# Eight half projections of the DeltaNet blocks moved into the filter stage, the second layer's modulations moved out of it

## The chip, the cores and the metric

The program runs on one core of a Trainium2 chip. Its engines are TensorE (PE in the profile; its weight loads are PEld), VectorE (DVE), ScalarE (ACT), GpSimd (POOL) and SyncE (SP), which here only issues DMAs. Each engine works through its own list of instructions in order, and semaphores tie the lists together. The metric is device time in microseconds (us) from start to end; lower is better.

## The reference, cut to what matters

Two layers over 1024 latent tokens of width 1024, with 256 context tokens in the first.

```python
def adaln_in(s, cvec, norm_g, mod_w, mod_b):
    m = jax.nn.silu(cvec) @ mod_w + mod_b
    shift, scale, gate = jnp.split(m, 3, axis=-1)
    return rmsnorm(s, norm_g) * (1.0 + scale) + shift, gate

def even_layer(x, ctx, ...):
    hx, gate_x = adaln_in(x, c_lat, norm_g, mod_w, mod_b)
    hc, gate_c = adaln_in(ctx, c_cx, norm_g, mod_w, mod_b)
    px = hx @ w_in
    pc = hc @ w_in
    ...
    dn_x, dn_c = bidir_gated_deltanet(px[..., OFF_DN:OFF_AB], ...)
    x_new = x + gate_x * ((jnp.concatenate([na_x, dn_x], axis=-1) * jax.nn.silu(px[..., OFF_Z:])) @ w_out)

def dn_prepare(qkv, ab, conv_w, a_log, dt_bias):
    t = jax.nn.silu(dwconv(qkv, conv_w)).astype(jnp.float32)
    ...

def hyena_layer(s, cvec, ...):
    h, gate = adaln_in(s, cvec, norm_g, mod_w, mod_b)
    ...
    filt = hyena_filters(s.shape[1], fw1, fb1, ff1, fw2, fb2, ff2, fw3)
```

The DeltaNet has four heads with a q, a k and a v block of 128 columns each: twelve column blocks of `w_in`, numbered 0 to 3 (q), 4 to 7 (k), 8 to 11 (v). k and v are also projected for the context tokens. The modulation `m` of a layer depends on `c` alone: a vector of 3072 numbers from a 1024 by 3072 matrix. The Hyena filters depend on weights alone.

## The kernel before

**Stages.** `start` (0 to about 378 us of the profile) computes the spectra of the Hyena filters, 16 of them, two for each column block `cb`: `filter_pair` multiplies (`fh`), scales and normalises; `filter_block` folds (`fp`, `ft`, `ff`) and transposes (`fx`); `filter_spectrum` makes the DFT on PE (`fb`) and stores the result (`G` to `g_d`). In the same stage the first layer's modulations (`em`), the normalised input h of tokens 0 to 511 and of the context, and at its end h of tokens 512 to 1023 are made. `project` (to about 740 us) makes the DeltaNet and attention projections: `gates` (`ab`), then for each head i `dn_front`, the gate block `zblock`, and for i = 1, 2 `dn_substitute` of the head before. Then come the DeltaNet scan (`dn_scan`, tiles `pa`, `pb`), attention, the output projection and the second layer.

**What sets the order.** Up to the end of the first part of `project` a scheduler orders the instructions of each engine by its own estimates; work in `high_priority(offset=-LOW)` is put where it leaves a hole. From the scan on, the matmuls are pinned in program order. All plain loads and stores stand on SP's one queue, and a DMA that waits holds up those behind it. POOL issues accumulating DMAs.

**Exact multiplication.** A weight block of 512 KB is loaded (`_raw`), split in `load_split` into a rounded part `hi` (a cast on ACT) and a remainder `lo`, and `gemm` takes three matmuls for each of eight slices of the contraction: 24 matmuls, of 512 columns for half of the latent tokens and of 256 for the context. With `add=True` the remainder is made by ACT (a negated copy) and an accumulating DMA from POOL (L154 to L156), otherwise by a subtraction on DVE. The buffers `wraw`, `whi` and `wlo` have two copies each.

**The modulation block.** `mod_block` (`em` and `om`, twelve blocks each) loads two halves of 512 KB, makes eight 32x256 matmuls into `_ps`, copies to `_p`, and for j below 8 transposes twice (`_t`) and reduces on DVE into `cols`; for j from 8 on one matmul (`_g`), an addition and a store to `gate_d`. Before, the twelve `om` blocks stand among the work of low priority in `start`, after eight `zblock`s; their loads use `wraw`, `whi` and `wlo`. `cols1` and `gate_d[1]` are first read after the scan.

**The DeltaNet block.** `dn_block` splits its weights, multiplies for tokens 0 to 511, 512 to 1023 and (k, v) the context, copies each result to `pad` on ACT (L654), and convolves on DVE (L658 to L664). `pad` (`dpad`) has two copies; POOL clears its margins (L650). `dn_front` goes on with transposes (`ktp`, `vtp`, `qtp`), norms, `kT`, products `kk`, `aq`, `R` (L719 to L729), the weights `W` on ACT and DVE (L734 to L744) and stores `lsc_d`. For group t0 and direction d of head i these are called `R0_4_1` and so on.

**The substitution and the levels.** `dn_substitute` loads `Lb` from `lsc_d`, does 31 dependent pairs of instructions on POOL (L763, L765) and stores `xsc_d` (L768, L769). `dn_tiles` loads `X` and `U`, and `dn_levels` begins with the matmuls `y1`. Of head 0 both stand in `project`; PE's list has `y1_0_0` between the projections of other heads.

Of the kernel before, what the change touches and what calls it, by code (L numbers as in the profile page):

```python
# [20 lines left out]
P = 128  # L21
# [40 lines left out]
class Kernel:  # L62
# [116 lines left out]

    def mod_setup(self, pool):  # L180

        nc, ap = self.nc, self.ap
        c0 = pool.tile([P, KT, 2], F32, name="c0")
        nc.sync.dma_start(c0, ap["cT"])
        c1 = pool.tile([P, KT, 2], F32, name="c1")
        self.cT = pool.tile([P, KT, 32], F32, name="cT")
        nc.vector.memset(self.cT, 0.0)
        nc.scalar.activation(c1, c0, AF.Tanh, scale=0.5)
        nc.vector.tensor_scalar_mul(c0, c0, 0.5)
        nc.vector.scalar_tensor_tensor(self.cT[:, :, 0:2], c1, 1.0, c0, ALU.add, ALU.mult)  # L190
        self.sel = pool.tile([P, 1], F32, name="sel")
        nc.sync.dma_start(self.sel, ap["sel"])
        self.mbias, self.mgain = {}, {}
        for name in ("em", "om"):
            self.mbias[name] = pool.tile([P, 24], F32, name=name + "_b")
            nc.sync.dma_start(self.mbias[name], ap[name + "_bcol"])
            self.mgain[name] = pool.tile([P, KT], F32, name=name + "_gc")
            nc.sync.dma_start(self.mgain[name], ap[name + "_g"])

    def mod_block(self, pool, name, j, cols, row, psp=None):  # L200

        nc, ap = self.nc, self.ap
        ps = self.psg.tile([P, 512], F32, name=f"{name}_ps{j}", tag="g")
        for i in range(2):
            b = 2 * j + i
            wp, tag = ((self.wraw, "wraw"), (self.wsp, "whi"), (self.wsp, "wlo"))[b % 3]
            w = wp.tile([P, 4, 256], F32, name=f"{name}_w{b}", tag=tag)
            nc.sync.dma_start(w, ap[name + "_w"][j][:, 4 * i:4 * i + 4, :])
            for k in range(4):
                nc.tensor.matmul(ps[32 * k:32 * k + 32, 0:256], self.cT[:, 4 * i + k, :], w[:, k, :],  # L210
                                 start=i == 0, stop=i == 1)
        part = pool.tile([P, 256], F32, name=f"{name}_p{j}", tag="mod_p", bufs=2)
        (nc.scalar.copy if psp is None else nc.vector.tensor_copy)(part, ps[:, 0:256])
        if j < 8:
            ps = self.psg.tile([P, 512], F32, name=f"{name}_t{j}", tag="g") if psp is None else \
                psp.tile([P, 512], F32, name=f"{name}_t{j}", tag="tp")
# [5 lines left out]
        else:  # L222
            ps = self.psg.tile([P, 512], F32, name=f"{name}_g{j}", tag="g")
            nc.tensor.matmul(ps[0:1, 0:256], self.sel, part, start=True, stop=True)
# [30 lines left out]
    def run(self):  # L255
# [61 lines left out]
    def start(self, st, sh, h):  # L317
# [90 lines left out]
    def project(self, h, wab):  # L408

        nc, ap = self.nc, self.ap  # L410
        with ExitStack() as st:
# [6 lines left out]
            with ExitStack() as s1:  # L418
# [153 lines left out]
    def gates(self, h, wab):  # L572
# [1384 lines left out]
```

## Time and profile before

| what | us |
|---|---|
| three runs | 1900.15, 1907.99, 1911.63 |
| their median | 1907.99 |
| the profiled execution's own time | 1902.58 |
| its span, first to last instruction | 1900.8 |
| PE busy in the span | 1734.8 |
| DVE busy in the span | 1417.5 |
| ACT busy in the span | 842.6 |
| POOL busy in the span | 582.4 |

A span is what the trace covers; some 1.8 us lie around it. A busy PE is not PE at its peak, since each matmul is counted from its issue to its modelled end, and these overlap. Rows of the chain of waits give a start, a duration and the instruction that the end of the program depended on there; rows of the timeline have start, duration, engine, line, operation, output and inputs; tables by stage give each engine's busy time and, in brackets, its instructions, then the granted clock of PE (1.00 is full), the busy share of the DMA engines and GB/s.

### The profile page before, as it was taken

Reading aid. Unit: us, or ns where it says so; the run is one execution under the profiler, and the core shown is the slowest. Engines: PE = TensorE matmul, PEld = TensorE weight load, DVE = VectorE, ACT = ScalarE, POOL = GpSimd, SP = SyncE. Lnnn points to the kernel's source line nnn. Section 1 sums busy time; section 2 is a strip of 40 time slices with the busy share of each in tenths; the row PEclk is TensorE's granted clock in tenths of the full one; section 3 lists DMA queues with packets and bytes.
Section 4 is the critical chain, followed back from the end, with each engine's and each line's share of the span. In section 5 each row is a group of like instructions: output and inputs, shape, how many; then the busy total and the mean of one; then the engine's idle time right before and its main releaser. Section 6 shows DMA issues by size and latency. Waiting matters only on the chain.

```text
span 1900.8 us, 30378 instructions
## 1 busy us (share of the span) xinstructions
PE 1734.8 (91%) x11124; PEld 1408.9 (74%) x11124; DVE 1417.5 (75%) x2847; ACT 842.6 (44%) x1830; POOL 582.4 (31%) x860
## 2 busy tenths in 40 slices
PE   6799988899998997999988899889999999999898
PEld 2366755688886775878877787778788788888686
DVE  5899988756677834555566565759999989999876
ACT  4557574444535432333344444544343434434321
POOL 0665554310193865721035401330000000000410
PEclk9889997999997998999999999999999999999999
DMA  8545455222424557454589863543433432443344
GB/s 287 167 117 158 136 187 170 107 73 103 149 94 116 163 173 229 145 131 155 158 230 230 227 192 85 185 113 93 121 108 83 105 104 72 113 128 106 108 131 139
DMA packets 162912, 270.53 MB, mean 142 GB/s; under 512 B 76953, under 2 KB 98985, under 8 KB 160714
## 3 DMA queue, kind: packets, MB, share of 16 engines
q1 hardware_dynamic: 152538, 230.83, 38.4%
q0 software_dynamic: 10224, 37.75, 10.2%
q8 instruction: 88, 1.44, 0.3%
q14 instruction: 62, 0.51, 0.1%
HBM read 192.50 MB, written 76.03 MB: 141 GB/s over the span
## 4 chain that ended last, share of the span: by engine, by line
PE 59%; DVE 21%; DMA 8%; POOL 4%; ACT 4%; issue 3%; SPq 1%; DVEq 0%; ACTq 0%; POOLq 0%
PE hx L116 6%; PE fo L116 4%; PE hg L116 3%; PE pa L116 3%; PE hu L116 2%; PE nk L116 2%; PE nv L116 2%; PE nq L116 2%; PE pq L116 2%; DVE ff L1169 2%; PE z L116 2%; PE dn L112 2%; PE dn L110 2%; PE dn L111 2%; PE pv L116 2%
## 5 line engine op out<-in xcount | busy, mean ns | idle before, releaser
L763 POOL TENSOR_TENSOR sub<-Lb,Xb 80x31 f32<-80x31 f32 (+15 forms) x124 | 87.2, 703 | 67.4 <-DMA Lb<-lsc_d 39.7
L116 PE MATMUL hx<-h1h,w1x_lo 128*128 128x512 f32 x256 | 101.0, 395 | 0.3 <-DMA w1x_lo<-in_w 0.3
L116 PE MATMUL hx<-h1l,w1x_hi 128*128 128x512 f32 x256 | 101.1, 395 | 0.0
L116 PE MATMUL hx<-h1h,w1x_hi 128*128 128x512 f32 x256 | 100.9, 394 | 0.0
L112 PE MATMUL dn<-hh,wdn_lo 128*128 128x512 f32 (+1 forms) x256 | 95.0, 372 | 0.9 <-DVE wdn_lo L105 0.9
L110 PE MATMUL dn<-hh,wdn_hi 128*128 128x512 f32 (+1 forms) x256 | 94.7, 370 | 0.0
L111 PE MATMUL dn<-hl,wdn_hi 128*128 128x512 f32 (+1 forms) x256 | 94.6, 370 | 0.0
L660 DVE SCALAR_TENSOR_TENSOR dacc<-dpad,convw,dacc 128x1024 f32<-128x1024 f32 (+1 forms) x80 | 75.9, 977 | 21.1 <-ACT dacc L658 20.2
L765 POOL TENSOR_TENSOR Xb<-Xb,sub 80x31 f32<-80x31 f32 (+15 forms) x124 | 82.9, 668 | 9.1
L1060 ACT ACTIVATE pr<-pr,st 128x640 f32<-128x640 f32 (+1 forms) x64 | 51.3, 802 | 54.1 <-DVE st L1059 54.0
L121 PE MATMUL pt<-ident,pr 128*128 128x128 f32 x304 | 46.4, 278 | 11.0 <-ACT pts L1073 6.7
L112 PEld LDWEIGHTS dn<-hh,wdn_lo 128*128 128x128 f32 x256 | 48.7, 190 | 9.8 <-DVE wdn_lo L105 1.3
L1180 ACT COPY fx<-fx_ps 128x512 f32<-128x512 f32 (+1 forms) x96 | 43.4, 484 | 27.9 <-PE fx_ps L121 24.6
L116 PEld LDWEIGHTS hx<-h1h,w1x_lo 128*128 128x128 f32 x256 | 48.1, 188 | 9.5 <-DMA w1x_lo<-in_w 0.7
L121 PE MATMUL fx_ps<-ident,ff 128*128 128x128 f32 x288 | 49.9, 299 | 5.7 <-ACT fx L1180 3.6
L1289 PE MATMUL fh<-fhh,w3s 128*128 128x512 f32 x64 | 38.2, 599 | 18.6 <-DVE fh L1291 18.6
L116 PEld LDWEIGHTS hx<-h1h,w1x_hi 128*128 128x128 f32 x256 | 48.1, 188 | 9.0
L116 PEld LDWEIGHTS hx<-h1l,w1x_hi 128*128 128x128 f32 x256 | 48.2, 188 | 8.9
L111 PEld LDWEIGHTS dn<-hl,wdn_hi 128*128 128x128 f32 x256 | 48.8, 191 | 8.0 <-issue 0.5
L110 PEld LDWEIGHTS dn<-hh,wdn_hi 128*128 128x128 f32 x256 | 48.8, 191 | 7.4
L121 PEld LDWEIGHTS pt<-ident,pr 128*128 128x128 f32 x304 | 36.3, 141 | 22.4 <-ACT pts L1073 9.3
L1313 POOL TENSOR_TENSOR fp<-fh,fh 128x1024 f32<-128x1024 f32 x16 | 39.4, 2461 | 42.4 <-ACT fh L1299 42.4
(576 smaller groups left out, 5920.1 us busy)
## 6 DMA issues: line engine op xcount, KB each, us to landing
hG<-g_d SPq DMA_DIRECT2D x16, 1088.0 KB
g_d<-G SPq DMA_DIRECT2D x16, 1024.0 KB
em_w<-in_em_w SPq DMA_DIRECT2D x24, 512.0 KB
om_w<-in_om_w SPq DMA_DIRECT2D x24, 512.0 KB
wz_raw<-in_w0z SPq DMA_DIRECT2D x16, 512.0 KB
w1x_raw<-in_w SPq DMA_DIRECT2D x16, 512.0 KB
w1x_lo<-in_w POOLq DMA_DIRECT2D x16, 512.0 KB, 7.6
wdn_raw<-in_w0dn SPq DMA_DIRECT2D x12, 512.0 KB
```

What stands on the lines that cost most here:

```text
L110: nc.tensor.matmul(ps, wh, xh, start=start, stop=False)
L111: nc.tensor.matmul(ps, wh, xl, start=False, stop=False)
L112: nc.tensor.matmul(ps, wl, xh, start=False, stop=stop)
L116: ins = self.nc.tensor.matmul(*args, **kw)
L121: ins = self.nc.tensor.transpose(out, x, self.ident)
L660: nc.vector.scalar_tensor_tensor(acc[:, t0:t0 + n], pad[:, o + j:o + j + n], cw[:, blk, j:j + 1], acc[:, t0:t0 + n], ALU.mult, ALU.add)
L763: nc.gpsimd.tensor_tensor(tv, Lb[:, j + 1:, j:j + 1].broadcast_to([80, m, c]), Xb[:, j:j + 1, 0:c].broadcast_to([80, m, c]), ALU.mult)
L765: nc.gpsimd.tensor_tensor(Xb[:, j + 1:, 0:c], Xb[:, j + 1:, 0:c], tv, ALU.subtract)
L1060: nc.scalar.activation(pr[:, :n], pr[:, :n], AF.Exp, bias=st[:, 0:1], scale=-1.0, accum_out=st[:, 1:2])
L1180: nc.scalar.copy(out[:, j0:j0 + m, :].rearrange("p a b -> p (a b)"), ps[:, :m * P])
L1289: nc.tensor.matmul(ps, ws[:, od, :], hh[:, sl], start=True, stop=False)
L1313: nc.gpsimd.tensor_tensor(pp[:, :L], hf[:, :L], hb[:, :L], ALU.add)
```

## The change

In `start`, the twelve `om` modulation blocks leave the work of low priority, and eight new `dn_early` take their place, for blocks 7, 11, 3, 6, 10, 2, 9 and 1 in this order: each loads and splits the block's weights (`we`), multiplies tokens 0 to 511 (`de`), copies the result on ACT (`dt`) and stores it in DRAM (`dne_d`). In `dn_block` these eight blocks drop the first of their segments and load it from `dne_d` into `pad` instead; their weights are loaded and split there as before. The `om` blocks are made in `project`, four after each of the first three `dn_front`s, with `X0`, `X1` and `U0` of the pool `bd` as buffers of their weights, with PSUM from `psb`. The small tiles of the modulations move to a pool that lives through `project`.

```diff
+DN_EARLY = (7, 11, 3, 6, 10, 2, 9, 1)
...
-    def mod_block(self, pool, name, j, cols, row, psp=None):
+    def mod_block(self, pool, name, j, cols, row, tags, psp=None):
...
-        ps = self.psg.tile([P, 512], F32, name=f"{name}_ps{j}", tag="g")
+        ps = self.psm.tile([P, 512], F32, name=f"{name}_ps{j}", tag=self.psm_tag)
         for i in range(2):
             b = 2 * j + i
-            wp, tag = ((self.wraw, "wraw"), (self.wsp, "whi"), (self.wsp, "wlo"))[b % 3]
+            wp, tag = tags[b % len(tags)]
...
+        self.dne_d = {i: scratch(f"dne{i}", [P, 512]) for i in DN_EARLY}
...
-        self.mod_setup(mp)
+        self.mod_setup(sh)
...
                         for zb in Z_EARLY:
                             self.zblock(h, zb, (0,), add=True)
-                        for j in range(12):
-                            self.mod_block(mp, "om", j, self.cols1, self.gate_d[1:2, :])
+                        for blk in DN_EARLY:
+                            self.dn_early(h, blk)
...
+                self.psm, self.psm_tag = self.psb, "t"
                 for i in range(HEADS):
                     self.dn_front(h, i)
+                    for j in range(4 * i, min(4 * i + 4, 12)):
+                        self.mod_block(self.dtmp, "om", j, self.cols1, self.gate_d[1:2, :],
+                                       ((self.bd, "X0"), (self.bd, "X1"), (self.bd, "U0")))
...
+    def dn_early(self, h, blk):
+
+        ps = self.gemm(self.load_split(self.ap["w0dn"][blk], f"we{blk}", add=True), h, 0, 512, f"de{blk}")
+        t = self.ev.tile([P, 512], F32, name=f"dt{blk}", tag="ev")
+        self.nc.scalar.copy(t, ps)
+        self.nc.sync.dma_start(self.dne_d[blk], t)
...
         segs = [(0, 512, 2), (512, 512, 514)] + ([(L, LC, L + 6)] if with_ctx else [])
+        if blk in DN_EARLY:
+            segs = segs[1:]
+            nc.sync.dma_start(pad[:, 2:514], self.dne_d[blk])
```

The scheduler moves other instructions with these. Three places show it. The names are those of tiles: `fh7_3_1` is the last filter product of the stage, `fb` and `fx` belong to spectra, `de2` and `de9` are early projections of blocks 2 and 9.

PE near the end of the filter stage, before:

```order
L1290 MATMUL fh7_3_1_3373<-fhl_200,w3s_7_3204 128x512
L116 MATMUL fb25_1_3196<-fx5_1_0_2998,dft_ccn_287 128x128 x2
L116 MATMUL fb06_0_1_3313<-fx6_0_1_3115,dft_b0_275 128x256
L116 MATMUL fb06_0_1_3313<-fx6_0_1_3115,dft_b1_277 128x256
L121 MATMUL fx6_1_1_ps0_3269<-ident_63,ff6_1_1_3256 128x128 x4
L210 MATMUL om_ps9_1082<-om_w18_1083,cT_159 32x256 x4
L210 MATMUL om_ps9_1082<-om_w19_1089,cT_159 32x256 x4
```

The same place on PE after the change:

```order
L1310 MATMUL fh7_3_1_3425<-fhl_211,w3s_7_3256 128x512
L112 MATMUL de2_1099<-hl0_201,we2_hi_1094 128x512
L113 MATMUL de2_1099<-hh0_200,we2_lo_1095 128x512
L111 MATMUL de2_1099<-hh0_200,we2_hi_1094 128x512
L112 MATMUL de2_1099<-hl0_201,we2_hi_1094 128x512
L113 MATMUL de2_1099<-hh0_200,we2_lo_1095 128x512
L117 MATMUL fb06_0_1_3365<-fx6_0_1_3167,dft_b0_286 128x256
L117 MATMUL fb06_0_1_3365<-fx6_0_1_3167,dft_b1_288 128x256
```

Behind the last `fh`, three of twelve `om` blocks stood before; now the rest of `de2` and all of `de9` and `de1` stand there, 53 matmuls of 512 columns.

DVE at the end of head 0's part of `dn_front`, before (`W0_4_1` is the last tile that head 0's substitution waits for):

```order
L739 TENSOR_TENSOR Wi0_4_1_4375<-W0_4_1_4369,masks_3760 128x512
L740 TENSOR_TENSOR Wi0_4_1_4375<-aq0_4_4344,Wi0_4_1_4375 128x512
L742 TENSOR_TENSOR W0_4_1_4369<-W0_4_1_4369,masks_3760 128x512
L105 TENSOR_TENSOR wdn2_lo_5273<-wdn2_raw_5270,wdn2_hi_5272 128x1024
L744 SCALAR_TENSOR_TENSOR W0_4_1_4369<-kk0_4_4339,beta_3850,W0_4_1_4369 128x128 x4
```

The same place on DVE after the change:

```order
L759 TENSOR_TENSOR Wi0_4_1_4427<-W0_4_1_4421,masks_3812 128x512
L684 SCALAR_TENSOR_TENSOR dacc1_4808<-dpad1_4777,dacc1_4808 128x1024
L760 TENSOR_TENSOR Wi0_4_1_4427<-aq0_4_4396,Wi0_4_1_4427 128x512
L762 TENSOR_TENSOR W0_4_1_4421<-W0_4_1_4421,masks_3812 128x512
L713 MEMSET ss2_5256 128x2
L106 TENSOR_TENSOR wdn2_lo_5380<-wdn2_raw_5377,wdn2_hi_5379 128x1024
L221 TENSOR_REDUCE cols1_138<-om_t7_5059 128x4
L764 SCALAR_TENSOR_TENSOR W0_4_1_4421<-kk0_4_4391,beta_3902,W0_4_1_4421 128x128 x4
```

The reduction of modulation block 7 now stands ahead of the last step of `W0_4_1`, and the last convolution step of block 1 has come between its first steps.

PE ahead of the first level of head 0, before (`dn11` is a projection, `y1_0_0` the first product of the levels):

```order
L110 MATMUL dn11_1024_5816<-hh2_194,wdn11_hi_5756 128x256
L111 MATMUL dn11_1024_5816<-hl2_195,wdn11_hi_5756 128x256
L112 MATMUL dn11_1024_5816<-hh2_194,wdn11_lo_5757 128x256
L116 MATMUL y1_0_0_6170<-U0_0_6150,X0_0_6148 32x32 x4
L729 MATMUL R1_4_1_4891<-gT_3861,gsel_3882 128x512
L116 MATMUL y1_0_0_6170<-U0_0_6150,X0_0_6148 32x32 x16
```

The same place on PE after the change:

```order
L113 MATMUL dn3_512_5999<-hh1_3660,wdn3_lo_5991 128x512
L739 MATMUL kk1_4_4941<-kT1_4853 128x128 x4
L745 MATMUL aq1_4_4946<-dacc1_4808,kT1_4853 128x128 x4
L749 MATMUL R1_4_0_4951<-gT_3913,gsel_3934 128x512
L117 MATMUL y1_0_0_6261<-U0_0_6241,X0_0_6239 32x32
L749 MATMUL R1_4_1_4969<-gT_3913,gsel_3934 128x512
L117 MATMUL y1_0_0_6261<-U0_0_6241,X0_0_6239 32x32 x19
```

Block 3's matmuls have moved ahead of `y1_0_0`; from `R0_4_1` to `y1_0_0` PE had 220 matmuls of 512 columns and now has 148, with five `om` blocks among them.

More of the change, by code (lines that the diff above doesn't have):

```diff
@@ L177, in gemm, with mod_setup @@
         return ps
-    def mod_setup(self, pool):
+    def mod_setup(self, sh):
         nc, ap = self.nc, self.ap
-        c0 = pool.tile([P, KT, 2], F32, name="c0")
+        pool = self.pool(sh, "mc", side="right")
+        c0 = self.small.tile([P, KT, 2], F32, name="c0", tag="c0", bufs=1)
         nc.sync.dma_start(c0, ap["cT"])
-        c1 = pool.tile([P, KT, 2], F32, name="c1")
+        c1 = self.small.tile([P, KT, 2], F32, name="c1", tag="c1", bufs=1)
         self.cT = pool.tile([P, KT, 32], F32, name="cT")
@@ L214, in mod_block @@
         if j < 8:
-            ps = self.psg.tile([P, 512], F32, name=f"{name}_t{j}", tag="g") if psp is None else \
+            ps = self.psm.tile([P, 512], F32, name=f"{name}_t{j}", tag=self.psm_tag) if psp is None else \
                 psp.tile([P, 512], F32, name=f"{name}_t{j}", tag="tp")
@@ L222, in mod_block @@
         else:
-            ps = self.psg.tile([P, 512], F32, name=f"{name}_g{j}", tag="g")
+            ps = self.psm.tile([P, 512], F32, name=f"{name}_g{j}", tag=self.psm_tag)
             nc.tensor.matmul(ps[0:1, 0:256], self.sel, part, start=True, stop=True)
@@ L330, in start @@
         self.ev = self.pool(sh, "ev", bufs=3, side="right")
+        tags = (self.wraw, "wraw"), (self.wsp, "whi"), (self.wsp, "wlo")
+        self.psm, self.psm_tag = self.psg, "g"
         self.hpool(sh, h, 0, 512)
@@ L341, in start @@
                     fil = hid, *self.filter_setup(fc)
-                self.mod_block(mp, "em", j, self.cols0, None, pst)
+                self.mod_block(mp, "em", j, self.cols0, None, tags, pst)
             xs = self.load_x(0)
@@ L348, in start @@
                         for j in range(8, 12):
-                            self.mod_block(mp, "em", j, None, self.gate_d[0:1, :])
+                            self.mod_block(mp, "em", j, None, self.gate_d[0:1, :], tags)
                         for zb in Z_EARLY:
                             self.zblock(h, zb, (0,), add=True)
-                        for j in range(12):
-                            self.mod_block(mp, "om", j, self.cols1, self.gate_d[1:2, :])
+                        for blk in DN_EARLY:
+                            self.dn_early(h, blk)
                 if cb == X2_AT:
```

## The prediction

> **What bounds the kernel now.** I read the chain of waits first. It runs through three stretches that this change touches: the filter stage to 378 us, `project` to about 740 us, and inside it a detour from PE to DVE, DMA and POOL. Then I took the tables by stage, to see which engine is short in each. The first table is `project`: from 400 to 550 us.
>
> ```profile
> core 0: us, PE busy (x) PEld busy (x) DVE busy (x) ACT busy (x) POOL busy (x), PEclk, DMA share, GB/s
> 400.00:450.00 50.00, 50.00 (x268) 42.76 (x267) 30.76 (x37) 26.47 (x62) 0.51 (x9) 1.00 0.22 72
> 450.00:500.00 50.00, 50.00 (x259) 41.15 (x258) 36.82 (x63) 25.68 (x52) 0.34 (x6) 1.00 0.31 100
> 500.00:550.00 50.00, 49.10 (x258) 41.33 (x257) 39.33 (x56) 27.16 (x70) 30.36 (x39) 1.00 0.43 135
> ```
>
> PE is never idle there and at full clock: matmuls taken out of this stretch shorten it, until something else is reached. That something is head 0's way through the substitution, in the chain of waits:
>
> ```profile
> 378.35 8.21 PE ab L582 x39
> ...
> 503.14 0.44 PE R L729
> 503.61 1.15 ACT W L734 x4
> ...
> 508.60 1.04 DVE W L744 x4
> ...
> 509.67 2.47 DMA lsc_d<-W
> ...
> 513.73 3.58 DMA Lb<-lsc_d
> ...
> 518.30 1.15 POOL sub L763
> ...
> 573.36 4.23 DMA xsc_d<-Lb
> ...
> 580.52 2.05 DMA U<-xsc_d
> ```
>
> The first `ab` is the start of `project`. From `R0_4_1` on PE (503.1) to the landing of U (582.6) lie 79.5 us in which no projection takes part: ACT, DVE and DMA for 15 us, 55 us of POOL pairs, and again DMA. PE's next rows, in the timeline and then by stage, show what waits for it:
>
> ```profile
> 575.88 0.28 PE L111 MATMUL dn<-hl,wdn_hi 128*128 128x256 f32 x1
> 576.00 0.28 PE L112 MATMUL dn<-hh,wdn_lo 128*128 128x256 f32 x1
> 580.15 0.22 PE L116 MATMUL y<-U,X 32*32 32x32 f32 x2 [3.87 <-DMA U<-xsc_d]
> 582.62 0.41 PE L116 MATMUL y<-U,X 32*32 32x32 f32 x6 [2.25 <-DMA U<-xsc_d]
> ...
> 582.00:602.00 20.00, 17.25 (x186) 13.56 (x187) 14.59 (x27) 14.40 (x43) 0.17 (x3) 0.50 0.58 177
> 602.00:612.00 10.00, 10.00 (x50) 8.29 (x49) 8.21 (x12) 4.74 (x18) 4.96 (x6) 1.00 0.11 18
> ```
>
> PE stands from 576.3 to 582.6, already 6.3 us, and then runs 20 us at half clock. So a PE that comes to `y1_0_0` earlier only waits longer. In the filter stage the tables are:
>
> ```profile
> 131.00:245.00 114.00, 105.08 (x543) 80.48 (x546) 107.20 (x238) 73.42 (x137) 60.62 (x78) 0.96 0.55 155
> 245.00:344.00 99.00, 84.29 (x560) 58.10 (x553) 84.74 (x214) 57.27 (x118) 47.50 (x59) 0.86 0.48 162
> 344.00:378.00 34.00, 25.78 (x183) 21.33 (x182) 24.36 (x45) 13.84 (x34) 13.29 (x9) 0.90 0.30 109
> ```
>
> The first row holds most of the eight z blocks, the second the `om` blocks, the third the tail. DVE is busy 94% and 86%. The cuts are starts of `fp`, which each filter block has once:
>
> ```profile
> 131.45 2.68 POOL L1313 TENSOR_TENSOR fp<-fh,fh 128x1024 f32<-128x1024 f32 x1
> ...
> 244.85 2.38 POOL L1313 TENSOR_TENSOR fp<-fh,fh 128x1024 f32<-128x1024 f32 x1 [0.30 <-ACT fh L1299]
> ...
> 344.03 2.37 POOL L1313 TENSOR_TENSOR fp<-fh,fh 128x1024 f32<-128x1024 f32 x1 [4.79 <-ACT fh L1299]
> ```
>
> Six blocks took 113.4 us beside z (18.9 each), five took 99.2 beside `om` (19.8 each): the pace did not follow the filler.
>
> **The change part by part.** Prices first. A matmul of 512 columns advances PE by 0.23 us and one of 256 by 0.12 (the second from the two `dn` rows above, 575.88 and 576.00); the rest from the chain, the timeline and the view by tile:
>
> ```profile
> 502.33 0.23 PE dn L112
> ...
> 264.78 1.07 PE L210 MATMUL om_ps<-om_w,cT 128*32 128x256 f32 x16
> 268.03 0.38 PE L218 MATMUL om_t<-ident,om_p 128*128 128x128 f32 x2
> ...
> L224 PE MATMUL om_g<-om_p,sel x8: 377/378/505, 321.6 to 347.5; 128*1 128x256 f32 x8
> ```
>
> One early projection is 24 x 0.23 = 5.5 us of PE, eight are 44.2 us. An `om` block is 1.07 (its eight instructions have 16 records) and 0.38 for either transposes or `_g`, 1.45 us; twelve are 17.4 us. So 44.2 us leave `project` and 17.4 enter it: net 26.8 us of PE out, and the same into the filter stage.
>
> (1) From the start of `project` to `R0_4_1`, counted in the two orders: 72 matmuls of 512 columns fewer (3 x 24, blocks 9, 1 and 6): -16.6. Four of 256 columns fewer: -0.5. Seven `om_ps` and six `om_t`: 7 x 1.07 + 6 x 0.38 = +9.8. `R0_4_1` comes 7.3 us earlier.
>
> (2) Its chain gets longer. On DVE the last step of `W0_4_1` now stands behind the reduction of `om_t7`. On PE, between `R0_4_1` and the end of `om_t7`, lie 23 matmuls of 256 columns, 6 of 512, two pairs of transposes, `om_ps7` and two transposes of `ktp1`: 2.8 + 1.4 + 0.8 + 1.1 + 0.4 = 6.5 us. With 0.44 for R and an estimated 0.2 for the small reduction the last step starts 7.1 us after R, where it was 5.5 (503.14 to 508.60): about +2. On POOL the memset of `U0` (buffer of the `om` weights) now stands just before the substitution's stores, not at the start: +1, by the memset of `Xb`:
>
> ```profile
> 575.87 0.94 POOL L757 MEMSET Xb<- 80x1024 f32 x1 [1.95 <-DMA xsc_d<-Xb]
> ```
>
> So `y1_0_0` moves by -7.3 + 2 + 1 = -4.
>
> (3) From `R0_4_1` to `y1_0_0` PE loses another 72 matmuls, 16.6 us, and gets five `om_ps`, two `om_t`, four `om_g` and four matmuls of 256: +8.1. These 8.5 us go into PE's wait for U: PE comes at 576.3 - 7.3 - 8.5 = 560.5, U at 582.6 - 4, and the wait grows from 6.3 to about 18. Worth 0.
>
> (4) From `y1_0_0` to the scan, PE has 48 matmuls of 512 fewer (block 3, block 7 and block 11 have moved ahead): up to -11. They are missing almost entirely between `kT3` and `R3_4_1`, where 52 filler matmuls become 3. There PE waits already:
>
> ```profile
> 714.85 1.16 PE L719 MATMUL kk<-kT 128*128 128x128 f32 x8 [1.23 <-ACT W L734]
> 717.41 1.67 PE L725 MATMUL aq<-dacc,kT 128*128 128x128 f32 x8 [1.41 <-DVE Wi L740]
> ...
> 721.64 0.79 PE L729 MATMUL R<-gT,gsel 40*128 40x512 f32 x1 [1.23 <-ACT W L734]
> 724.81 0.80 PE L116 MATMUL nk<-hh,wn_hi 128*128 128x512 f32 x1 [2.38 <-ACT nvst L524]
> ```
>
> Head 3's ACT and DVE steps bind there. From 0 to -11, I take -5.
>
> (5) The filter stage: 26.8 us more PE. Nearest row: the z region, where 8 fillers of the same 24 matmuls were spread over 127 us; now 8 fall on about 110. Per early block ACT gets a negated copy, a cast and a copy, POOL one DMA issue; DVE, which a z block costs 0.68 us, gets nothing.
>
> ```profile
> L110 PE MATMUL z<-hh,wz_hi x64: 387/394/792, 112.0 to 238.7; 128*128 128x512 f32 x64
> L493 DVE SCALAR_TENSOR_TENSOR zt<-zt,z x8: 669/677/686, 130.2 to 241.8; 128x512 f32<-128x512 f32 x8
> ...
> L156 POOL DMA_DIRECT2D wz_lo<-in_w0z x8: 856/881/1014, 90.4 to 205.9; - x8
> DMA to landing us min/median/max: 5.6/7.9/10.5
> ```
>
> At z's pace five blocks take 94.5 us, not 99.2: -5. If PE binds: seven of the eight z blocks, 40 us, lie in the first row of that table, so a filter block's own PE time is (105 - 40)/6 = 10.8 us, and 5 x 10.8 + 32 (the 5.8 early projections ahead of the last `fh`) at 92% is 93 us; no loss before 344. In the tail 53 matmuls (12.2 us) replace three `om` blocks (4.4): 25.8 busy of 34 becomes 33.6, so up to +8. From -5 to +13 (should half of the 26.8 not be hidden), I take +2.
>
> (6) The loads. SP gets 24 loads of 512 KB and eight of 256 KB in `project`, and as many `om` loads leave the filter stage, where eight `we_raw` and eight stores come. In `project` the `om` loads share three buffers, so each waits on SP for a matmul of the block before, with `wdn` loads and the `lsc_d` stores queued behind it. In the order of PE the second half of an `om_ps` comes some 5 us after its load can start. From issue to landing 512 KB took, by the chain of waits at two places:
>
> ```profile
> 1193.09 4.02 DMA ex<-xa_d
> ...
> 15.55 6.75 DMA em_w<-in_em_w
> ```
>
> So 0 to 1.8 us for each of six tight blocks ahead of `om_ps8`: 0 to +11, I take +2. The load of `dne_d` into `pad` waits for the same DVE step as the store of `qT` ahead of it: 0. Less work for ACT (eight copies of a 512-column result gone, twelve of `om` come) is off the path.
>
> Sum: -4 (1, 2, 3) - 5 (4) + 2 (5) + 2 (6) = -5 us. Against the profiled execution's 1902.6 that is 1897.6; the median of the runs shown lies 5.4 above it, which would make 1902.6. The forecast goes by the middle of the two starting points, 1905: 1900.
>
> [...] PE's clock was 0.86 in the `om` region and 0.96 in the z region, and fell to 0.50 behind the wait at 576. [...]
>
> **The rivals.**
>
> (A) Part of the saving, as above: 1890 to 1911.
>
> (B) It comes through. The early projections fill PE in the filter stage and hold its clock, so its pace is z's (-5 in (5)); nothing is added in (2), so that `y1_0_0` moves by the whole -7; and PE is what binds up to the scan (-11 in (4)): 1905 - 23 = 1882. For it: the 18.9 against 19.8 us per block. Against it: head 3's steps on ACT and DVE, for which PE already waits.
>
> (C) Nothing. The tail of the filter stage takes what `project` gives: +8 from (5), +2 from (6), -9 from (1) to (4): 1906, inside the range of (A). Here the change still does what it says.
>
> (D) Slower: SP is the place. If each of the twelve `om` blocks lets PE wait for its second load, 2.7 us each (6.75 less some 4 us of other matmuls), `project` gets +32 and the sum becomes -9 + 2 + 32 = +25: 1930. It ends slower than before from about 0.6 us per block. For it: the three buffers, and `om_ps7` ahead of head 0's last DVE step. Against: DMA engines are 22 to 43% busy there.
>
> **How the numbers follow.** (A) 0.50, (B) 0.23, (C) 0.17, (D) 0.10. The measurement can tell about 1%, 19 us, from no change: faster means under 1889, which is (B), 0.23; slower means over 1927, most of (D), 0.09; the rest, 0.68, is (A) and (C). The range, 1881 to 1920, leaves out half of (B) and most of (D), and takes in the ends of (4), (5) and (6) around (A).
>
> **What would show it.** Step (1): from the first `ab` to `R0_4_1` about 117 us, not 125. (2): the DMA of `lsc_d` 8.5 us behind R. (3): PE idle ahead of `y` about 18 us, and half clock behind it. (4): PE's idle time between `kT3` and `R3_4_1` grows as the filler goes. (5): the first `ab` at 373 to 391 us, likeliest 380. (6): PE waiting for `om_w`, 2 us in all. From the scan to the end the program should keep its length. The forecast is wrong if U lands more than 10 us earlier relative to `ab`, or if PE waits for `om_w` for more than 10 us.

## The result, and the profile after

| | before | changed |
|---|---|---|
| median, lowest to highest (9 runs each, same chip), us | 1905.51, 1899.94 to 1911.63 | 1919.59, 1911.64 to 1921.95 |
| ratio, 95% interval | | 1.0066, 1.0046 to 1.0086 |
| profiled execution: own time, span, us | 1902.58, 1900.8 | 1911.64, 1909.9 |

The change made the kernel slower by 14 us, where 5 us of gain were forecast. The profiled execution of the changed kernel is the fastest of its nine, so its trace shows 9.1 of the 14 us.

The program was cut at four marks: `fp` at 131 us, up to which the two do not differ; the first `ab`, where `project` starts; the first `y`; and the `pa` of the scan that waits for `vg`. The two marks of before that the prediction did not quote, from its timeline (start, duration, engine, line, operation, and in brackets the idle time before it and what ended that):

```profile
378.11 0.48 PE L582 MATMUL ab<-hh,wab 128*32 128x512 f32 x1
...
748.18 1.22 PE L116 MATMUL pa<-vg,ktm 128*128 128x128 f32 x4 [6.00 <-ACT vg L880]
```

The same marks in the timeline of the changed kernel:

```profile
131.34 2.68 POOL L1333 TENSOR_TENSOR fp<-fh,fh 128x1024 f32<-128x1024 f32 x1
...
384.85 0.48 PE L592 MATMUL ab<-hh,wab 128*32 128x512 f32 x1
...
590.23 0.28 PE L117 MATMUL y<-U,X 32*32 32x32 f32 x2 [16.90 <-DMA U<-xsc_d]
592.85 1.27 PE L117 MATMUL y<-U,X 32*32 32x32 f32 x38 [1.61 <-DMA U<-xsc_d]
...
756.44 1.22 PE L117 MATMUL pa<-vg,ktm 128*128 128x128 f32 x4 [5.25 <-ACT vg L900]
```

| stretch, us | before | changed | difference | forecast |
|---|---|---|---|---|
| `fp` to first `ab` | 246.7 | 253.5 | +6.8 | +2 |
| `ab` to `y` | 202.0 | 205.4 | +3.4 | -4, and 2 of loads |
| `y` to `pa` | 168.0 | 166.2 | -1.8 | -5 |
| `pa` to the end | 1152.6 | 1153.5 | +0.9 | 0 |

`project` lost 26.8 us of PE's work, by the prediction's count, and got longer. The first sign is in front of `y`: PE stands 16.9 us, about as forecast. What happened ahead of it shows in the timelines of R, `W`, SP's issues and POOL. Before:

```profile
503.07 0.50 PE L729 MATMUL R<-gT,gsel 40*128 40x512 f32 x1
...
504.94 0.32 SPq L746 DMA_DIRECT2D lsc_d<-W  x1
...
507.82 1.62 SPq L755 DMA_DIRECT2D Lb<-lsc_d  x4
509.67 0.34 SPq L746 DMA_DIRECT2D lsc_d<-W  x1
...
512.52 1.60 SPq L755 DMA_DIRECT2D Lb<-lsc_d  x4
...
517.56 0.25 POOL L763 TENSOR_TENSOR sub<-Lb,Xb 80x31 f32<-80x31 f32 x1 [13.11 <-DMA Lb<-lsc_d]
```

and in the changed kernel:

```profile
504.51 0.50 PE L749 MATMUL R<-gT,gsel 40*128 40x512 f32 x1
...
507.01 0.80 SPq L210 DMA_DIRECT2D om_w<-in_om_w  x2
507.91 0.38 SPq L766 DMA_DIRECT2D lsc_d<-W  x1
...
512.39 1.12 DVE L764 SCALAR_TENSOR_TENSOR W<-kk,beta,W 128x128 f32<-128x128 f32 x4
515.11 1.62 SPq L775 DMA_DIRECT2D Lb<-lsc_d  x4
...
517.48 0.37 SPq L766 DMA_DIRECT2D lsc_d<-W  x1
...
522.11 1.60 SPq L775 DMA_DIRECT2D Lb<-lsc_d  x4
...
526.10 0.34 POOL L783 TENSOR_TENSOR sub<-Lb,Xb 80x31 f32<-80x31 f32 x1 [15.78 <-DMA Lb<-lsc_d]
```

Read it from the top. The first of the two stores is issued 0.9 us behind two `om_w` loads and lands 7.2 us later (507.91 to 515.11, where `Lb` could be loaded), against 2.9 before (504.94 to 507.82). SP stands at the first load of `Lb` until then, some 3.5 us, and the second store stands behind it: `W0_4_1` is ready at 513.5 and is stored at 517.48. From R to the first `sub`, which is called the way below, it takes 21.6 us, where it took 14.5. Of these 7.1 us the later `W0_4_1` makes 2.4, the wait of the second store for SP 3.9 and its landing 1.8 (4.6 for 2.9); from the load of `Lb` to `sub` it is 1.0 shorter.

Second, the waits of all engines from 560 to 620 us of the changed kernel (us in all, times, longest), and SP's own in 380 to 620:

```profile
PE y L117 <- DMA U<-xsc_d: 18.5, 2, 16.9
...
ACT W L754 <- DMA lsc_d<-W: 16.3, 1, 16.3
POOL sub L783 <- DMA Lb<-lsc_d: 14.5, 1, 14.5
...
SPq L804 <- DMA xsc_d<-Xb: 16.1, 1, 16.1
```

PE is not alone in waiting. SP stands 16.1 us at the first load of `X` from `xsc_d`; ACT stands as long, for a store of `W`; and POOL, done with head 0, waits 14.5 us for head 1. SP's timeline says why:

```profile
569.48 0.32 SPq L761 DMA_DIRECT2D at_d<-Wi  x1
586.01 1.07 SPq L804 DMA_DIRECT2D X<-xsc_d  x2
...
589.26 0.40 SPq L766 DMA_DIRECT2D lsc_d<-W  x1
```

Head 1's store of `W` stands behind head 0's loads of `X` and `U`. On PE the first `y` stands just ahead of head 1's last R, and the front of head 2 (`ktp`) behind the others:

```profile
590.44 0.79 PE L749 MATMUL R<-gT,gsel 40*128 40x512 f32 x1
...
594.04 0.69 PE L701 MATMUL ktp<-ident,dacc 128*128 128x128 f32 x2
```

The filter stage, in the table by stage of the changed kernel:

```profile
core 0: us, PE busy (x) PEld busy (x) DVE busy (x) ACT busy (x) POOL busy (x), PEclk, DMA share, GB/s
246.00:350.00 104.00, 94.84 (x497) 75.43 (x496) 81.60 (x196) 67.34 (x123) 48.32 (x62) 0.95 0.48 132
350.00:385.00 35.00, 30.06 (x214) 26.35 (x213) 27.52 (x51) 16.48 (x39) 15.47 (x16) 1.00 0.34 128
```

The slip is not in the tail (34.8 us, 34.1 before). The five filter blocks ahead of it took 104.4 us, 20.9 each, against 19.8 beside `om`.

### The profile page after: what moved, and what is told of

Its sections match the earlier page's. It is cut to its first block, busy times and chain, and to the rows that moved or that the text cites. A ratio compares the mean times of both kernels' runs of the same rounds, so it can differ in the third digit from the quotient of the medians.

```text
span 1909.9 us, 30455 instructions
## 1 busy us (share of the span) xinstructions
PE 1728.6 (91%) x11124; PEld 1403.7 (73%) x11124; DVE 1422.3 (74%) x2847; ACT 855.7 (45%) x1846; POOL 582.4 (30%) x868
## 5 line engine op out<-in xcount | busy, mean ns | idle before, releaser
L783 POOL TENSOR_TENSOR sub<-Lb,Xb 80x31 f32<-80x31 f32 (+15 forms) x124 | 83.3, 672 | 70.0 <-DMA Lb<-lsc_d 41.3
L111 PE MATMUL dn<-hh,wdn_hi 128*128 128x512 f32 (+1 forms) x192 | 69.4, 362 | 0.0
L113 PE MATMUL dn<-hh,wdn_lo 128*128 128x512 f32 (+1 forms) x192 | 69.4, 362 | 0.0
L112 PE MATMUL dn<-hl,wdn_hi 128*128 128x512 f32 (+1 forms) x192 | 69.4, 361 | 0.0
L1313 ACT ACTIVATE fjk<-fh 128x1024 bf16<-128x1024 f32 x32 | 34.0, 1063 | 42.2 <-DVE fh L1311 39.0
L117 PE MATMUL hu<-h1h,w1u_hi 128*128 128x512 f32 x128 | 51.2, 400 | 0.8 <-ACT hpu L1660 0.8
L117 PE MATMUL fo<-owo_lo,fyh 128*128 128x512 f32 x112 | 45.9, 410 | 6.1 <-POOL owo_lo L106 5.9
L117 PE MATMUL hu<-h1h,w1u_lo 128*128 128x512 f32 x128 | 50.9, 397 | 0.0
L117 PE MATMUL hu<-h1l,w1u_hi 128*128 128x512 f32 x128 | 50.8, 397 | 0.0
```

Source lines behind the costliest of these rows:

```text
L111: nc.tensor.matmul(ps, wh, xh, start=start, stop=False)
L112: nc.tensor.matmul(ps, wh, xl, start=False, stop=False)
L113: nc.tensor.matmul(ps, wl, xh, start=False, stop=stop)
L117: ins = self.nc.tensor.matmul(*args, **kw)
L783: nc.gpsimd.tensor_tensor(tv, Lb[:, j + 1:, j:j + 1].broadcast_to([80, m, c]), Xb[:, j:j + 1, 0:c].broadcast_to([80, m, c]), ALU.mult)
L1313: nc.scalar.activation(junk, t[:, :L], AF.Square, accum_out=ss[:, od % 2:od % 2 + 1])
```

## The experiments

All times are medians; "before" is the kernel before in runs on the same chip in the same session. The changed kernel itself ran in the first session alone, so a variant is compared with it by its ratio (1.0066), or by marks of the profiles, of which there is one for each kernel.

| run | us | before | ratio, 95% interval |
|---|---|---|---|
| de_third | 1916.1 | 1908.3 | 1.0045, 1.0023 to 1.0067 |
| om_one_load | 1906.9 | 1908.3 | 0.9992, 0.9971 to 1.0013 |
| om_only | 1918.7 | 1908.3 | 1.0053, 1.0033 to 1.0073 |
| head0_first | 1903.4 | 1908.3 | 0.9979, 0.9963 to 0.9995 |
| om_pool | 1912.7 | 1905.7 | 1.0042, 1.0026 to 1.0058 |
| de_nolo | 1914.4 | 1905.7 | 1.0040, 1.0021 to 1.0060 |
| h0_three | 1913.1 | 1905.7 | 1.0045, 1.0026 to 1.0065 |
| h0_ompool | 1901.1 | 1905.7 | 0.9979, 0.9960 to 0.9998 |
| r_first | 1906.0 | 1905.3 | 1.0005, 0.9987 to 1.0022 |
| de_split | 1925.0 | 1905.3 | 1.0097, 1.0070 to 1.0124 |
| h0_ompool_r | 1900.6 | 1905.3 | 0.9968, 0.9948 to 0.9988 |
| h0_three_r | 1887.0 | 1905.3 | 0.9899, 0.9875 to 0.9922 |
| rx_pool | 1897.2 | 1904.3 | 0.9952, 0.9934 to 0.9970 |
| h0_three_rx | 1880.4 | 1904.3 | 0.9867, 0.9840 to 0.9893 |
| before_r_first | 1915.7 | 1904.3 | 1.0057, 1.0035 to 1.0080 |
| before_rx | 1908.7 | 1906.2 | 1.0010, 0.9993 to 1.0028 |

The stretch up to the `fp` of the first mark, which no edit touches, took 126.5 to 131.7 us in these profiles, so marks are compared from the profile's own `fp` or first `ab`.

**What costs the filter stage its 6.8 us.** de_third takes away PE's part; it leaves out two thirds of the products:

```diff
-        ps = self.gemm(self.load_split(..., add=True), h, 0, 512, f"de{blk}")
+        w = self.load_split(..., add=True)
+        for k in range(KT):
+            self.nc.tensor.matmul(ps, w[int(k == KT - 1)][:, k, :], h[0][0][:, k, :], ...)
```

> Each early projection keeps its load, its ACT copies, its POOL transfer and its store, but issues 8 of its 24 matmuls (the products with hl, and all but one with we_lo, are left out, so these blocks are coarser): 29.5 us less PE in the filter stage; the order in project is that of the changed kernel. Theory M (the early blocks' matmuls stand on PE ahead of the filters' own steps): the first ab comes back from 384.8 to 377 to 380 us, and the time falls by 5 to 7 us against the changed kernel, to about 1913. Rival N (what costs is the other work of an early block: ACT's copies, POOL's transfer, the loads): the first ab stays at 384 to 386 and the time at 1919.

Its `fp` and first `ab`:

```profile
131.06 2.66 POOL L1336 TENSOR_TENSOR fp<-fh,fh 128x1024 f32<-128x1024 f32 x1
...
385.19 0.78 PE L592 MATMUL ab<-hh,wab 128*32 128x512 f32 x1
```

From `fp` to `ab` it takes 254.1 us. Theory M falls: 29.5 us less PE leave the stage as long as it was. (The time, 1916.1, lies between the two theories; the mark tells them apart.) de_nolo leaves PE's work and takes away the remainder, so its early blocks are coarser:

```diff
+        raw = self.wraw.tile(...); self.nc.sync.dma_start(raw, self.ap["w0dn"][blk])
+        w = self.wsp.tile(...); self.nc.scalar.copy(w, raw)
+        for k in range(KT):
+            for n, i in enumerate((0, 1, 0)):
+                self.nc.tensor.matmul(ps, w[:, k, :], h[0][i][:, k, :], ...)
```

> Each early projection keeps its first load, one ACT copy, all 24 matmuls and its store; its we_lo is gone, so POOL issues no accumulating transfer and ACT makes no negated copy (the product with we_lo is replaced by a second one with we_hi). Theory N1 (POOL's queue, which waits for the negated copy, or that copy on ACT, holds the filters): from the fp at 131 us to the first ab 247 to 250 us instead of 253.5, and the time 3 to 6 us less than the changed kernel's. Theory N2 (the loads and stores, or the order that the filters' own steps get): 252 to 255 us, and the time as the changed kernel's, 1917 to 1920.

```profile
126.89 2.69 POOL L1340 TENSOR_TENSOR fp<-fh,fh 128x1024 f32<-128x1024 f32 x1
...
375.40 0.78 PE L592 MATMUL ab<-hh,wab 128*32 128x512 f32 x1
```

This is 248.5 us, 5.0 less than the changed kernel, as theory N1 has it. The changed kernel's view of the tile `we_lo` has what POOL spends, eight issues of 0.88 us, and waits at them:

```profile
L157 POOL DMA_DIRECT2D we_lo<-in_w0dn x8: 842/878/881, 227.1 to 339.1; - x8
...
  POOL we_lo L157: 9.9, 3
```

de_split lets POOL subtract instead (`load_split` without `add=True`), which removes the same copy and the same transfer and adds POOL work, eight subtractions that are estimated at 2.4 us each by POOL's `fp` of the same 128x1024 (median 2.38 us).

> The early blocks' we_lo is computed by POOL as a difference instead of a negated copy on ACT and an accumulating transfer: 8 x 2.4 us more work for POOL, 8 copies less for ACT, 4 MB less to move. Theory N1a (POOL stands at the issue of the transfer until ACT's negated copy is done, or the transfer lands late): from the fp at 131 us to the first ab 247 to 250 us instead of 253.5, and 1914 to 1916. Theory N1b (POOL's time as such, whose work the filters wait for): 254 to 258 us, and 1919 to 1923.

```profile
127.64 2.69 POOL L1333 TENSOR_TENSOR fp<-fh,fh 128x1024 f32<-128x1024 f32 x1
...
387.00 0.48 PE L592 MATMUL ab<-hh,wab 128*32 128x512 f32 x1
```

This is 259.4 us, and 1925.0: theory N1b, and beyond its range. POOL's time costs, since the filters' folds stand in the same list; what ACT's copy and the transfer cost beside it was not separated. One reservation: the scheduler orders the stage anew in each variant, and om_only below, with no early blocks and no `om`, took 249.3 us, 2.7 more than before with `om`. h0_ompool and h0_ompool_r, whose edits differ in `project` alone, took 253.2 and 256.0. Differences of 3 us here need no cause of their own.

**What the om blocks cost in `project`.** om_one_load takes 23 of their loads away (all read `self.om_one`, loaded for b = 0), om_pool has 16 of them issued by POOL:

```diff
-            nc.sync.dma_start(w, ap[name + "_w"][j][:, 4 * i:4 * i + 4, :])
+            (nc.gpsimd if name == "om" and j < 8 else nc.sync).dma_start(w, ap[name + "_w"][j][:, 4 * i:4 * i + 4, :])
```

> The om blocks all read one tile of weights that is loaded once, so 23 of 24 loads of 512 KB are gone (the modulations of the second layer come out other than they should); matmuls, reductions and their order on PE stay. Theory Q (the om transfers and their places on SP lengthen the way from R0_4_1 to the first sub, 21.6 us in the changed kernel and 14.4 before): the way is 15 to 17.5 us, R0_4_1 comes at ab + 117.5 instead of 119.7, y1_0_0 at ab + 197 to 200 instead of 205.4, and the time falls by 4 to 7 us, to about 1914. Rival O (the order on DVE, or the loads of dne_d): the way stays at 20 to 22 us, and the time at 1919.

> The 16 loads of om blocks 0 to 7 are issued by POOL, which has almost nothing to do ahead of the first sub, instead of SP; nothing else is changed, and the bytes are the same. Theory Q1 (SP's order: the stores and loads of head 0's chain wait on SP behind loads that wait for their buffers): from R0_4_1 to the first sub 15 to 18 us, as with one load (17.3), and 1907 to 1912. Theory Q2 (the transfers themselves: om loads fill the DMA engines, 249 GB/s against 135, and the small transfers of the chain land late): 20 to 22 us, and 1917 to 1920.

The rows of om_one_load:

```profile
501.46 0.32 SPq L772 DMA_DIRECT2D lsc_d<-W  x1
...
504.27 0.32 SPq L781 DMA_DIRECT2D Lb<-lsc_d  x1
...
507.40 0.43 SPq L150 DMA_DIRECT2D wdn_raw<-in_w0dn  x1
507.93 0.37 SPq L772 DMA_DIRECT2D lsc_d<-W  x1
...
512.66 1.60 SPq L781 DMA_DIRECT2D Lb<-lsc_d  x4
```

The first store lands in at most 2.8 us again, the second goes out 0.6 us after `W` is there and takes 4.7, now behind a load of weights. The way is 17.2 us (theory Q), `y` comes at `ab` + 201.5, and the time is 0.7%, 14 us, under the changed kernel's ratio: without these loads the kernel is level with the one before. That is more than the 4 to 7 us expected, and more than the 5.4 us that its profile gains from `ab` to `pa`; where the rest lies these traces do not show. The rows of om_pool:

```profile
507.35 0.33 SPq L210 DMA_DIRECT2D om_w<-in_om_w  x1
507.78 0.38 SPq L766 DMA_DIRECT2D lsc_d<-W  x1
...
513.12 0.31 SPq L775 DMA_DIRECT2D Lb<-lsc_d  x1
...
525.96 0.25 POOL L783 TENSOR_TENSOR sub<-Lb,Xb 80x31 f32<-80x31 f32 x1 [16.64 <-DMA Lb<-lsc_d]
```

The first landing takes 5.3 us and the way 21.5, which is in the range of Q2. But the run does not separate the two theories. The sixteen loads were all issued by 500.6; the three next to the stores belong to blocks 8 and 9, which om_pool leaves on SP, one of them 0.4 us ahead of the first store. So SP's order at this place is nearly that of the changed kernel, and so are the bytes: the DMA share from 498 to 527 us is 0.79 here, 0.74 in the changed kernel and 0.47 before. What om_one_load shows is the price of both together, the bytes and the places on SP. The time of om_pool fell to 1912.7, between the two theories: behind `y`, `pa` came at `ab` + 361.9 instead of 371.6. In this variant the scheduler had put R1_4_1 ahead of `y1_0_0`; that led to r_first.

om_only is the other half of the change alone (`DN_EARLY = ()`).

> No early projections; the om blocks alone move to project. The filter stage loses 17.4 us of PE, project has 17.4 more than before. Theories M and Q: first ab at 370 to 378 us; from R0_4_1 to the first sub 18 to 22 us; PE reaches y1_0_0 after U, so it does not wait there; the 44.2 us that project has more than in the changed kernel fill the 17 us wait ahead of y and some 10 us between kT3 and R3_4_1, the rest is paid: 1917 to 1928. Rival (nothing of the early projections reaches the end, their 44 us only fill waits): 1905 to 1912, no slower than before by more than the om loads.

The time came out as expected, 1918.7: moving `om` by itself costs 10 us against the kernel before, less than its 17.4 us of PE. Two of its marks did not: the first `ab` came at 379.8 us, not at 370 to 378, and the way took 23.2 us, not 18 to 22.

**Why PE's saving brings nothing behind `y`.** r_first pins two matmuls in program order:

```diff
+                if (hd, t0, d) == (1, 4, 1):
+                    self.tc.keep_in_program_order(ins)
...
+                    if self.pinned or (hd, d) == (0, 0):
+                        self.tc.keep_in_program_order(ins)
```

The first `ins` is R's matmul in `dn_front`, the second that of `y1`. rx_pool adds one line, in `dn_tiles`:

```diff
-                    nc.sync.dma_start(T[d][32 * b:32 * b + 32, :, 32 * b:32 * b + 32],
+                    (nc.sync if hd else nc.gpsimd).dma_start(T[d][32 * b:32 * b + 32, :, 32 * b:32 * b + 32],
```

> The changed kernel with one order fixed: R1_4_1 stands on PE ahead of y1_0_0 (in the changed kernel one y1_0_0 matmul stands just ahead of it); the transposes of head 2's k and v come ahead of y1_0_0 with it. Nothing else is changed. Theory H (what stands on PE behind its wait for U, head 1's last R and head 2's front, is what was lost between y and the scan): R1_4_1 at ab + 186 to 190 instead of 205.6, PE's wait ahead of y about 8 us instead of 16.9, the first sub of head 1 at ab + 222 to 226 instead of 227.5, the first pa at ab + 360 to 366 instead of 371.6, and 1908 to 1914. Rival K (the gain of om_pool behind y came from SP's shorter queue): pa at ab + 370 to 372, and 1917 to 1920.

> r_first with the sixteen loads of head 0's X and U from xsc_d issued by POOL, which has just stored xsc_d and then idles until head 1, instead of SP. Theory S (in the changed kernel SP stands at the first of these loads until POOL's store, 16.1 us, and the store of head 1's W stands behind it; ACT needs that W's buffer, and PE needs ACT): in r_first ACT waits 16.4 us for lsc_d<-W and PE 17.4 us ahead of head 2's ktp; both fall under 5 us, the first sub of head 1 comes at ab + 212 to 220 instead of 226.2, the first pa at ab + 352 to 360 instead of 364.8: 1895 to 1902. Rival (PE's order was all of it): 1904 to 1907.

In r_first PE's list did what was asked (R1_4_1 at `ab` + 189.7), but PE then stood behind ACT instead. Its waits from 560 to 620 us:

```profile
PE ktp L701 <- ACT W L756: 17.4, 1, 17.4
ACT W L756 <- DMA lsc_d<-W: 16.4, 1, 16.4
```

`pa` came at `ab` + 364.8, and the time, 1906.0, is better than expected. In rx_pool these two waits are down to 2.1 and 1.1 us, the first `sub` of head 1 comes at `ab` + 215.9, and

```profile
736.60 1.22 PE L117 MATMUL pa<-vg,ktm 128*128 128x128 f32 x4 [5.11 <-ACT vg L904]
```

This `pa` is at `ab` + 357.0, 14.6 us earlier than in the changed kernel, and the time is 1897.2. Theory S holds: it was not PE alone that waited for U but SP too, and through it ACT and head 1. Issuing these sixteen loads from POOL brought `pa` 7.8 us forward (`ab` + 357.0, 364.8 in r_first), since a load that waited no longer held up the store behind it. The kernel before with the same edits tells whose loss this is.

> The kernel before with y1_0_0 held behind R1_4_1. It asks how much of that loss the kernel before has itself: its wait ahead of y is 6.3 us against 16.9. If the loss grows with the wait: 1899 to 1904, so some 5 us of the 13.6 that r_first gained are older than the change. If it is as large as in the changed kernel: 1890 to 1896. If none of it is there: 1905.

> The kernel before with both edits of rx_pool: y1_0_0 held behind R1_4_1, and the sixteen loads of head 0's X and U on POOL. It asks how much of h0_three_rx's 24 us comes from the early blocks. Theory S: before_r_first's waits behind SP (7.0 us of ACT for lsc_d<-W, 8.7 us of PE ahead of head 2's ktp) go, so pa comes 5 to 9 us earlier than in before_r_first: 1906 to 1911, no faster than before, since without the early blocks PE is not early at y. Rival (the order alone is the gain, the early blocks add nothing): 1880 to 1890.

before_r_first was slower, 1915.7, which none of its three cases had. Yet its `pa` came at `ab` + 367.3, 2.8 us earlier than before; the loss lies behind `pa`, where it took 1169.6 us to the end and the kernel before 1152.6. before_rx is level with before in time, as expected, and its trace parts in the same way:

```profile
375.82 0.47 PE L582 MATMUL ab<-hh,wab 128*32 128x512 f32 x1
...
735.97 1.22 PE L116 MATMUL pa<-vg,ktm 128*128 128x128 f32 x4 [6.03 <-ACT vg L884]
```

Its `pa` is at `ab` + 360.2, 9.9 us earlier than before, and 1170.8 us follow. So of the 14.6 us that the order cost the changed kernel up to `pa`, the kernel before had already lost some 10. With the order released in both kernels, the change brings 3.2 us from `ab` to `pa` (357.0 against 360.2), less than the filter stage pays for it. The lead of rx_pool over before_rx in time, 11 us, lies behind `pa`, where neither has an edit. That stretch took 1152.6 to 1170.8 us in the profiles of all these kernels, least in the kernel before; in the two variants of the kernel before most of the difference is in attention (tile `pv`, 193 us for 182), where PE waits 10 us for `dx` (2.5 before). Whether the order ahead does this or one execution differs from the next, a single profile each does not show.

**Towards a faster kernel.** head0_first takes the early blocks of head 0 first (`DN_EARLY = (4, 0, 8, 5, 1, 9, 6, 2)`); h0_ompool adds om_pool's line, h0_ompool_r also r_first's pins. h0_three has three early blocks, `(4, 0, 8)`, and `om` back in the filter stage; h0_three_r lists the early blocks ahead of `om` and has the pins; h0_three_rx adds rx_pool's line.

> The early blocks are 4, 0, 8, 5, 1, 9, 6, 2: head 0 whole, then heads 1 and 2, so that head 0's chain starts earlier. Filter stage as in the changed kernel (first ab 383 to 387). PE has 8.5 us less ahead of R0_4_1. If head 0's way through POOL sets when y1_0_0 starts (theory U), y1_0_0 comes 6 to 9 us earlier against ab, at ab + 197 to 199; PE has 10.7 us more behind it than the changed kernel, of which the idle time between kT3 and R3_4_1 takes 5 to 10: 1912 to 1918. If it is not what sets the scan's start, the time is 1919 or more.

> head0_first (early blocks 4, 0, 8, 5, 1, 9, 6, 2) with the loads of om blocks 0 to 7 issued by POOL. Theory Q1: the way from R0_4_1 to the first sub falls from 18.1 to 14.5 to 16 us, and the time from 1903 to 1899 to 1901. Theory Q2: 18 us and 1903.

> h0_ompool with y1_0_0 held behind R1_4_1 in the order of PE, which moves some 20 us of other work (head 2's transposes and projections) ahead of y1_0_0. Theory H: PE's wait ahead of y falls from 15 to 0 to 5 us, the first pa comes at ab + 346 to 353 instead of 356.9, and 1891 to 1897. If only R1_4_1 itself mattered, which stood ahead of y already: 1900 to 1902.

> Only head 0's three blocks (4, 0, 8) are early, and the om blocks stand in the filter stage as before. Theory U (head 0's way through POOL, started earlier, is what moves the scan): R0_4_1 at ab + 109 to 111 (before 125.0), from it to the first sub 14 to 16 us, y1_0_0 at ab + 186 to 190 (before 202.0), first pa at ab + 354 to 360 (before 370.1); PE busy from the fp at 131 us to ab is that of the changed kernel, so ab slips by 3 to 7 us: 1894 to 1902. If the slip of the filter stage follows the number of early blocks and not PE (theory N1), ab slips by 2 to 3 us only. If U is not what binds: 1905 or more.

> h0_three with the three early blocks ahead of the om blocks in the filter stage's list, and y1_0_0 held behind R1_4_1. Theory: the tail of the filter stage (last fp to ab, 49.5 us in h0_three, 34.1 before) held the early blocks there; it falls to 35 to 42, so from the fp at 131 us to ab 248 to 254 us instead of 257; pa at ab + 350 to 357 instead of 361.8: 1894 to 1902. If the slip goes with the three blocks wherever they stand: 1905 or more.

> h0_three_r with the same sixteen loads on POOL. There PE waited 9.8 us ahead of head 2's ktp. Theory S: that wait goes, first sub of head 1 at ab + 203 to 208 instead of 210.5, pa at ab + 338 to 344 instead of 346.4: 1880 to 1884. Rival: 1886 to 1888.

head0_first was faster than expected (1903.4, and `y` at `ab` + 194.1). The way of h0_ompool did not shorten (18.3, as Q2 has it), though its 1901.1 is at the end of Q1's range. h0_ompool_r missed theory H (1900.6): `y` is held back to `ab` + 208.4, and PE waits 14 us later on, at `qtp`. h0_three missed as well: its early blocks stood in the tail, 351 to 382 us, and the stage took 257.0 us. With the list turned round, in h0_three_r, they stood at 241 to 286 us and the stage took 251.7; its 1887.0 is below the range that was expected. h0_three_rx is 1.3% faster than the kernel before; its `ab` and `pa`:

```profile
383.31 0.42 PE L591 MATMUL ab<-hh,wab 128*32 128x512 f32 x1
...
723.38 0.74 PE L117 MATMUL pa<-vg,ktm 128*128 128x128 f32 x4 [2.33 <-ACT vg L903]
```

From `ab` to `pa` it takes 340.1 us against 370.1 before. Of these 30 us before_rx has 9.9 without early blocks. The other 20 are more than the 16.6 us of PE work that three early blocks take out: head 0's chain starts earlier, with `R0_4_1` at `ab` + 109.9 where it was at 125.0. The filter stage pays 5.2 us for them (251.9 for 246.7).

## Why the prediction was wrong, step by step

The sign was wrong; the time (1919.6) lies at the upper end of the range, and that is in part luck: what the range held room for, a longer tail of the filter stage and PE waiting for `om_w`, did not come, and other losses took its place. Neither of the two signs that the prediction named for being wrong came either: U landed later and not earlier, and PE did not wait for `om_w`. Against the forecast the profile lost 5.4 us ahead of `y` (terms 1, 2 and 6), 4.8 in the filter stage (term 5), 3.2 from `y` to `pa` (terms 3 and 4) and 0.9 behind. The step that failed first is the price of the `om` loads in (6): they were priced by PE's wait for them, and what they do to head 0's stores on SP was put at nothing. Without the loads the kernel is level with the one before (om_one_load). In (6) and (3) the manner is the same: what stands behind a waiting instruction was counted on PE and not on SP's list.

- **(1), PE up to R0_4_1,** was forecast at `ab` + 117 and came at 119.7. With one load it came at 118.1, so 1.5 of the 2.7 us go with the loads.
- **(2) and (6), the way and the loads.** (2) gave DVE +2 and it took +2.4 (the last step starts 7.9 us behind R, 5.5 before). (6) asked what PE pays for the `om` loads, 0 to 11, and took 2; the views show no wait of PE for `om_w`. The price stood where the step itself had said the stores are queued: the first store of `lsc_d` landed late, and SP stood at the load of `Lb` with the second store behind it. The way took +7.1 in place of +2. The +1 for the memset of `U0` on POOL measured 1.7 from first `sub` to store.
- **(3), "worth 0".** The wait ahead of `y` was right, 16.9 for 18, and so was that PE's own 8.5 us end in it. That the same wait holds SP's store for head 1, ACT's next `W` and R1_4_1 behind `y1_0_0` was not looked at: at `pa` it cost 14.6 us (rx_pool). Some 10 of these the kernel before lost too (before_rx), so the change added about 5.
- **(4),** forecast -5 because head 3's ACT and DVE steps bind: -1.8. The reason holds for where the moved work went: PE's waits from `kT3` to `R3_4_1` grew from 4.4 to 14.7 us, nearly by the 11 that were taken out. But head 3 could come earlier: with head 1 released, the `pa` behind it came 14.6 us earlier.
- **(5), the filter stage,** was sized by PE and by the tail: +2, within -5 to +13; it was +6.8. The tail hardly grew (0.7 us), and PE had no part in it (de_third). The row that said so stood in the prediction, that the pace does not follow the filler; POOL's issue was named there and not priced. Without the remainder, whose transfer POOL issues, 5.0 of the 6.8 us go (de_nolo).
- **PE's clock.** Rival (B) had the early projections hold the clock of the filter stage, worth -5 in (5). The clock did rise over the five filter blocks (0.95, 0.86 before), and they got longer all the same (104.4 us, 99.2 before), since PE's speed was not what they waited for (de_third).
- **The rivals.** (C) put the loss into the tail, which grew by 0.7 us; (D) had the right thing, the `om` loads on SP, at the wrong price and victim: not PE waiting 2.7 us at each of twelve blocks, but one chain delayed once. Its counter-argument, DMA engines 22 to 43% busy, was read before the loads came: around the stores the share is 0.74.

What stays open: where the 5 us lie by which the median gap exceeds the gap of the profiles, why removing the loads or fixing the order gains 5 to 9 us more in the ratios than from `ab` to `pa` in the profiles, and what makes the stretch behind `pa` differ by up to 18 us between kernels that are the same there.

## What to carry to other kernels

When work leaves an engine that already waits, ask for every engine, the DMA-issuing one first, what stands in its list behind the same wait; here a saving arrived only when none of the next chain did (`pa` 14.6 us earlier in rx_pool). Make the same edit to the kernel before as well, since a loss that it uncovers can be an old one. Price bulk loads that are moved next to a latency chain by the landing times of the chain's small transfers (7.2 us for 2.9 here) and by what its queue holds behind them, not by the waits of the loads' own reader. Choose filler by what it puts into the lists that the stage's own chain runs through, and move early what starts the longest chain rather than what comes last.

## What was not expected of the hardware

The landing of one 256 KB store took 2.9 us with a 512 KB store issued 1.0 us ahead of it (before), 7.2 with two 512 KB loads issued 0.9 us ahead (changed), and 4.7 with a load of 512 KB issued 0.5 us ahead (507.40 and 507.93, the second store of om_one_load). And the clock: after its wait of 6.3 us before, PE ran at half clock (0.50) for 20 us; after 16.9 us in the changed kernel, for some 11. Windows of the changed kernel behind `y`:

```profile
594.00:598.00 4.00, 3.92 (x92) 2.90 (x89) 1.66 (x5) 3.74 (x12) 0.18 (x3) 0.50 0.43 56
598.00:602.00 4.00, 4.00 (x14) 3.09 (x13) 3.94 (x10) 3.94 (x13) 0.00 (x0) 0.59 0.81 285
602.00:606.00 4.00, 4.00 (x24) 3.42 (x23) 4.00 (x9) 2.17 (x8) 0.00 (x0) 1.00 0.62 235
```

PE is busy nearly without gap from 592.9 on and gets the full clock at about 601 (0.59 from 598 to 602). Before, a last gap of 1.5 us ends at 591.3, and the window from 598 to 602 still has 0.52. So the clock came back some 8 and some 10 us after the last gap of over 1 us, the longer time behind the shorter wait. That is not a fixed time: by the steps between matmuls of 512 columns, 0.43 us first and 0.23 then, it was 6 us in om_one_load (591.2 to 597.1) and 4 in h0_three_rx (580.1 to 584.4).
